# Stick-breaking attention: two key chunks' output products in one run, and transposed weights written over the untransposed ones

## The chip, the cores and the metric

The program runs on one core of one Trainium2 chip. The metric is the device time of one execution, in microseconds (us), given as the median of several runs. The profile shows five engines: PE (TensorE, whose weight loads are listed as PEld), DVE (VectorE), ACT (ScalarE), POOL (GpSimd) and SP (SyncE, which here only issues DMAs). Each engine runs its own list of instructions in the order in which the program was built.

## The reference, cut to what matters

The kernel computes two blocks, one after the other, on 2048 tokens of width 1024. The first block has a gated short convolution and then an attention layer whose weights break a stick; the second block has a pooling mixer and an attention over 256 selected keys per query. The change is in the first block's attention:

```
for blk in range(n_blocks):                       # 128 queries each
    z = einsum(q_blk, k[:kl]) * HEAD_DIM ** -0.5  # 8 heads of 64
    mask = arange(kl)[None, :] < q_pos[:, None]
    log_one_minus = where(mask, log_sigmoid(-z), 0.0)
    rev = cumsum(log_one_minus, axis=3, reverse=True)
    weights = exp(where(mask, z + rev, -inf))
    outs.append(einsum(weights, v[:kl]))
```

So the weight of a key is sigmoid(z) of that key times the product of sigmoid(-z) over all later keys that the query sees. The keys are therefore walked from the last one back to the first.

## The kernel before, in words

The work is written as Python generators, one for each phase: `phase_a` is the convolution, `phase_b` makes keys, values, queries and gates, `phase_c` is the stick-breaking attention, `phase_d` the projection after it, `phase_e` and `phase_e2` the second block's projections, `phase_f` its attention, `phase_g` the output. `merge` interleaves two generators: the one whose share of its own stated total is lowest goes next, so a smaller total makes a generator look further along and be called less often. `ahead` gives all that a generator emits a higher priority. What is written in this way goes through a scheduler, which sets the order on each engine; that order then is fixed. `phase_c(0)` (queries 0 to 1023) is merged with `phase_b(1)`, and `phase_c(1)` (queries 1024 to 2047) with `phase_d(0)`, `phase_e(0)` and `phase_e2`. Most of the work beside phase_c is the helper `lin`, whose matmuls L119, L120 and L121 stream 512 columns each.

In `phase_c`, p is a pair of heads, g a group of 512 queries, i one of its four blocks of 128 queries, and c a chunk of 512 keys, from g down to 0. nb is the number of 128-key pieces of a chunk: 4, or i+1 in the diagonal chunk c == g. For each (p, g, i, c), here called a chunk, and each head a of the pair:

- L533 and L534 (PE) make the scores z in one of two PSUM banks.
- L536 (ACT) writes sigmoid(z) into a buffer `s` of the ring `cs` (4 buffers before). In the diagonal chunk L538 and L541 (DVE) mask and form 1-s; elsewhere L543 (ACT) writes sigmoid(-z) into `e` of the ring `ce`.
- L546 (DVE) runs the product of `e` backwards over the keys, and starts from the last value of the chunk done before. L547 (DVE), and L549 (POOL) for one column, multiply it into `s`: these are the weights.
- L553 (PE) transposes `s` in nb pieces of 128x128 into a PSUM tile `tp`, and L555 (ACT) copies that into a buffer `wt` (ring of 3).

When both heads are copied, L561 (PE) adds the chunk's output products to the bank `o`: 2 nb matmuls, whose outputs lie in partitions 0 to 63 for the first head and 64 to 127 for the second. Each of them loads only 64 columns of stationary data (the values) and stands in the profile as two records, so a chunk of four pieces has 8 matmuls and 16 records. The helper `burst` lets the first of them wait for the last copy and gives them one priority, so that they tend to stand in one run. For each p, the groups g = 0, 1, 2, 3 have 4, 8, 12 and 16 chunks: 48 chunks in `phase_c(0)`, 112 in `phase_c(1)`, 160 in all.

At the end of a group L576 (DVE) multiplies `o` by the gate `sg`, and a DMA stores it to `ogd`. All `crf` names in the profile are buffers of the rings above; `crr` holds queries and keys.

Of the kernel before, what the change touches and what calls it, by code (L numbers as in the profile page):

```python
# [7 lines left out]
F32 = mybir.dt.float32  # L8
# [7 lines left out]
ALU = mybir.AluOpType  # L16
# [39 lines left out]
def merge(*gens):  # L56
    run(merged(*gens))
# [11 lines left out]
class Build:  # L69
# [434 lines left out]
    def phase_c(self, h):  # L504
        nc = self.nc
        if h == 0:
            self.c_rings()
        for p in range(4):
            for g in (2 * h, 2 * h + 1):
                gs = slice((g % 2) * CH, (g % 2 + 1) * CH)  # L510
                sg = self.turn("csg", 1)
                self.dma(sg, self.sg1[p][h][:, gs])
                q = [self.load_dup("cq", 3, self.qst[p][h], a, gs) for a in range(2)]
                kt, vt = {}, {}
                for c in range(g, -1, -1):
                    cs = slice((c % 2) * CH, (c % 2 + 1) * CH)
                    kt[c] = self.load_stack("ck", 4, self.kst[p][c // 2], cs)
                    if c == g or c % 2:
                        n = HT // P if c % 2 else HT // P // 2
                        v = self.turn("cv", 2)  # L520
                        self.dma(v[:, :n], self.vst[p][c // 2][: n * P, :].rearrange("(b p) d -> p b d", p=P))
                    vt[c] = v[:, c % 2 * 4 : c % 2 * 4 + 4]
                o = self.psum("o")
                for i in range(4):
                    qs = slice(i * P, (i + 1) * P)
                    prev = [None, None]
                    for c in range(g, -1, -1):
                        nb = i + 1 if c == g else 4
                        W = nb * P
                        wts = []  # L530
                        for a in range(2):
# [3 lines left out]
                            s = self.turn("cs", 4)  # L535
# [15 lines left out]
                            tp = self.psum("tp")  # L551
                            for j in range(nb):
                                nc.tensor.transpose(tp[:, j * P : (j + 1) * P], s[:, j * P : (j + 1) * P], self.ident)  # L553
                            wt = self.turn("wt", 3)
                            last = nc.scalar.copy(wt[:, :W], tp[:, :W])  # L555
                            wts.append(wt)
                        with self.burst(last) as first:
                            for j in range(nb):
                                for a in range(2):
                                    first(  # L560
                                        nc.tensor.matmul(  # L561
                                            o[a * 64 : (a + 1) * 64, qs],
                                            vt[c][:, j, a * 64 : (a + 1) * 64],
# [916 lines left out]
```

## Time and profile before

| what | value |
|---|---|
| median of 3 runs | 3356.41 us (3351.19 to 3359.43) |
| the profiled execution's own time | 3360.51 us |
| its span, first to last instruction | 3358.8 us |
| PE busy | 3212.6 us, 96% |
| DVE busy | 2249.0 us, 67% |
| ACT busy | 1501.3 us, 45% |
| POOL busy | 470.9 us, 14% |
| mean granted TensorE clock | 0.977 of full |

A busy PE here is a PE with a matmul in flight, and matmuls overlap: one of 512 columns lasts 0.39 us in the records, while the next starts 0.23 us after it. So the distance between starts is what a matmul costs, and the busy share does not show how much of it is useful.

### The profile page before, as it was taken

How to read it: one execution, taken by the hardware profiler on the slowest of the kernel's cores; microseconds unless marked ns; L12 is line 12 of the kernel's file. 1: busy time of each engine (PE TensorE's matmuls, PEld its weight loads, DVE VectorE, ACT ScalarE, POOL GpSimd, SP SyncE). 2: the span in 40 equal slices, each digit the busy share in tenths (PEclk: the TensorE clock that was granted, in tenths of full speed). 3: DMA queues.
4: the chain of work that ended last, by engine and by line, in shares of the span. 5: the costliest groups of instructions: out<-in, count | busy, mean ns of one | idle time of the engine just before them, and what ended most of it. 6: DMA issues, size and time to landing. Idle time of an engine off the chain costs nothing.

```text
span 3358.8 us, 49679 instructions
## 1 busy us (share of the span) xinstructions
PE 3212.6 (96%) x18050; PEld 2546.6 (76%) x18050; DVE 2249.0 (67%) x4516; ACT 1501.3 (45%) x2794; POOL 470.9 (14%) x584
## 2 busy tenths in 40 slices
PE   8999999999999999998899999889999999999997
PEld 7888888788878778776678887667877777666775
DVE  5344534545253878788888788798946878799741
ACT  4111421111232544465555555565365555776571
POOL 0000010000100000033312112331110143103002
PEclk9999999999999999997999999889999999999998
DMA  3111452424454455474456544554553265115115
GB/s 105 48 48 47 138 169 88 132 85 138 129 179 154 143 153 160 127 245 131 117 157 182 171 141 158 168 168 135 172 164 105 84 214 171 47 39 172 46 30 180
DMA packets 371683, 439.77 MB, mean 131 GB/s; under 512 B 25696, under 2 KB 271968, under 8 KB 371424
## 3 DMA queue, kind: packets, MB, share of 16 engines
q1 hardware_dynamic: 371424, 436.44, 42.1%
q8 instruction: 147, 2.41, 0.3%
q14 instruction: 112, 0.92, 0.1%
HBM read 309.46 MB, written 125.30 MB: 129 GB/s over the span
## 4 chain that ended last, share of the span: by engine, by line
PE 78%; DVE 13%; ACT 3%; issue 3%; DMA 2%; POOL 0%; SPq 0%; ACTq 0%; DVEq 0%; POOLq 0%
PE lin L119 11%; PE lin L120 10%; PE lin L121 10%; PE z L119 4%; PE z L120 4%; PE z L121 4%; PE o L561 4%; PE o L1221 3%; PE tp L553 3%; PE tp L1213 3%; PE tp L120 3%; PE tp L119 3%; PE tp L121 3%; DVE crf L546 2%; PE z L533 2%
## 5 line engine op out<-in xcount | busy, mean ns | idle before, releaser
L119 PE MATMUL lin<-act,fixedr 128*128 128x512 f32 x1488 | 597.4, 402 | 15.0 <-DVE x1r L597 7.9
L120 PE MATMUL lin<-act,fixedr 128*128 128x512 f32 x1488 | 595.2, 400 | 9.5 <-DVE act L618 7.2
L121 PE MATMUL lin<-act,fixedr 128*128 128x512 f32 x1488 | 592.2, 398 | 0.0
L104 ACT ACTIVATE fixedr<-fixed 128x512 fp32r<-128x512 f32 x294 | 185.9, 634 | 726.1 <-PE lin L120 263.2
L546 DVE TENSOR_TENSOR_SCAN crf<-crf 128x512 f32<-128x512 f32 (+3 forms) x320 | 354.6, 1116 | 74.0 <-ACT crf L543 71.4
L119 PEld LDWEIGHTS lin<-act,fixedr 128*128 128x128 f32 x1488 | 284.0, 191 | 80.3 <-DVE x1r L597 9.8
L120 PEld LDWEIGHTS lin<-act,fixedr 128*128 128x128 f32 x1488 | 283.8, 191 | 74.3 <-DVE act L618 10.0
L105 DVE TENSOR_TENSOR fixedr<-fixed,fixedr 128x512 fp32r<-128x512 f32 x294 | 203.5, 693 | 197.7 <-ACT fixedr L104 186.2
L121 PEld LDWEIGHTS lin<-act,fixedr 128*128 128x128 f32 x1488 | 283.7, 191 | 61.0 <-issue 0.2
L1162 DVE CUSTOM_DVE_ANT_0 fe<-z,masks 128x512 f32<-128x512 f32 (+3 forms) x320 | 188.3, 605 | 105.0 <-PE tp L1213 53.3
L119 PE MATMUL z<-act,fixedr 128*128 128x512 f32 x584 | 231.7, 397 | 9.3 <-ACT fixedr L104 9.3
L536 ACT ACTIVATE crf<-z 128x512 f32<-128x512 f32 (+3 forms) x320 | 175.3, 549 | 144.6 <-PE tp L553 109.8
L555 ACT COPY crf<-tp 128x512 f32<-128x512 f32 (+3 forms) x320 | 164.9, 532 | 156.0 <-PE tp L553 135.8
L120 PE MATMUL z<-act,fixedr 128*128 128x512 f32 x584 | 231.0, 396 | 0.0
L121 PE MATMUL z<-act,fixedr 128*128 128x512 f32 x584 | 230.9, 396 | 0.0
L549 POOL TENSOR_TENSOR crf<-crf 128x1 f32<-128x1 f32 x192 | 93.2, 487 | 928.8 <-ACT crf L536 732.5
L1176 ACT ACTIVATE fe<-fe,fixed 128x1024 f32<-128x1024 f32 (+7 forms) x192 | 189.7, 992 | 71.6 <-DVE fixed L1173 70.8
L1215 ACT COPY ff<-tp 128x512 f32<-128x512 f32 (+3 forms) x320 | 161.2, 523 | 127.2 <-PE o L1221 65.7
L883 DVE SCALAR_TENSOR_TENSOR sc<-ff,fixed,sc 128x512 f32<-128x512 f32 (+3 forms) x266 | 180.8, 702 | 52.3 <-ACT ff L876 50.5
L547 DVE TENSOR_TENSOR crf<-crf 128x511 f32<-128x511 f32 (+3 forms) x320 | 199.8, 630 | 10.7 <-PE lin L121 0.5
L1213 PE MATMUL tp<-fixed,fe 128*128 128x128 f32 x1088 | 181.8, 282 | 21.0 <-ACT fe L1176 16.4
L876 ACT ACTIVATE ff<-z 128x512 f32<-128x512 f32 (+3 forms) x304 | 158.2, 547 | 92.2 <-PE z L874 73.1
(346 smaller groups left out, 6541.5 us busy)
## 6 DMA issues: line engine op xcount, KB each, us to landing
fixed<-in_w_in_a_dram SPq DMA_DIRECT2D x128, 256.0 KB, 2.7
fixedr<-kept_w_out SPq DMA_DIRECT2D x64, 512.0 KB, 4.8
kept_w_in<-fixedr SPq DMA_DIRECT2D x46, 512.0 KB, 4.1
fixedr<-kept_w_in SPq DMA_DIRECT2D x46, 512.0 KB, 4.0
crr<-kst SPq DMA_DIRECT2D x80, 256.0 KB, 5.4
crr<-qst SPq DMA_DIRECT2D x64, 256.0 KB, 5.4
fixed<-x2d SPq DMA_DIRECT2D x64, 256.0 KB, 3.8
ffr<-q2s SPq DMA_DIRECT2D x128, 128.0 KB, 2.9
```

What stands on the lines that cost most here:

```text
L104: nc.scalar.activation(t[:, 0], raw, AF.Copy)
L105: nc.vector.tensor_tensor(t[:, 1], raw, t[:, 0].bitcast(F32), ALU.subtract)
L119: self.nc.tensor.matmul(ps[:, :n], whi[k], a, start=k == 0, stop=False)
L120: self.nc.tensor.matmul(ps[:, :n], whi[k], b, start=False, stop=False)
L121: self.nc.tensor.matmul(ps[:, :n], wlo[k], a, start=False, stop=k == nk - 1)
L536: nc.scalar.activation(s[:, :W], z[:, :W], AF.Sigmoid)
L546: nc.vector.tensor_tensor_scan(er, er, er, left, ALU.mult, ALU.min)
L547: nc.vector.tensor_tensor(s[:, : W - 1], s[:, : W - 1], e[:, 1:W], ALU.mult)
L883: nc.vector.scalar_tensor_tensor(sc[:, c0 : c0 + m], r[:, :m], w, sc[:, c0 : c0 + m], ALU.mult, ALU.add)
L1162: nc.vector.tensor_tensor_reduce(row[c0 // HT][:, c0 % HT : c0 % HT + m], z[:, :m], mb[:, c0 : c0 + m], 1.0, NEG, ALU.subtract, ALU.max, m ...
L1176: nc.scalar.activation(x, x, AF.Exp, bias=nbs, scale=sc, accum_out=den[:, u, hd : hd + 1])
L1213: nc.tensor.transpose(tp[:, j * P : (j + 1) * P], pe[a][k0 // HT][:, k0 % HT : k0 % HT + P], self.ident)
```

## The change

Each chunk's transposes, copies and output products are moved into a method `c_outputs`, which is called one chunk later, when the next chunk's scores and weights have been emitted (`c_behind` holds what is due). The copy L579 writes the transposed weights back into `s` itself, so the ring `wt` is gone and `cs` has 7 buffers. The output products are collected in `c_due` and issued for two chunks together, when g - c is odd or c is 0. The loads of the gate and of the values of a group are written behind the first chunk of that group. Two totals of the interleaving change: `phase_c(1)` from 260 to 230, and the last part of `phase_f` from 500 to 460.

```
-        f = self.at.tile([P, (4 + 4 + 3) * CH + 2 * HT + CH], F32, name="crf", tag="crf", bufs=1)
+        f = self.at.tile([P, (7 + 4) * CH + 2 * HT + CH], F32, name="crf", tag="crf", bufs=1)
...
-        for name, b, m in (("cs", 4, CH), ("ce", 4, CH), ("wt", 3, CH), ("csg", 1, CH), ("cv", 2, HT)):
+        for name, b, m in (("cs", 7, CH), ("ce", 4, CH), ("csg", 1, CH), ("cv", 2, HT)):
...
+        self.c_behind, self.c_out, self.c_due = None, {}, []
...
-                            s = self.turn("cs", 4)
+                            s = self.turn("cs", 7)
...
-                            tp = self.psum("tp")
-                            for j in range(nb):
-                                nc.tensor.transpose(tp[:, j * P : (j + 1) * P], s[:, j * P : (j + 1) * P], self.ident)
-                            wt = self.turn("wt", 3)
-                            last = nc.scalar.copy(wt[:, :W], tp[:, :W])
-                            wts.append(wt)
-                        with self.burst(last) as first:
-                            for j in range(nb):
-                                for a in range(2):
-                                    first(
...
+                            ws.append(s)
+                        if self.c_behind is not None:
+                            self.c_outputs(*self.c_behind)
+                        if (i, c) == (0, g):
+                            sg = self.turn("csg", 1)
+                            self.dma(sg, self.sg1[p][h][:, gs])
+                            for k in range(g, -1, -1):
+                                if k == g or k % 2:
...
+                        self.c_behind = h, p, g, i, c, ws, vt[c], sg
...
+    def c_outputs(self, h, p, g, i, c, ws, v, sg):
...
+        for s in ws:
+            tp = self.psum("tp")
+            for j in range(nb):
+                nc.tensor.transpose(tp[:, j * P : (j + 1) * P], s[:, j * P : (j + 1) * P], self.ident)
+            last = nc.scalar.copy(s[:, :W], tp[:, :W])
+        self.c_due += [(a, ws[a], j, v, c == g and j == 0, c == 0 and j == nb - 1) for j in range(nb) for a in range(2)]
+        if (g - c) % 2 or c == 0:
+            o = self.c_out[p, g]
+            with self.burst(last) as first:
+                for a, wt, j, v, begins, ends in self.c_due:
+                    first(
+                        nc.tensor.matmul(
...
+            self.c_due = []
+        if (i, c) == (3, 0):
+            nc.vector.tensor_tensor(sg, o, sg, ALU.mult)
+            self.dma(self.ogd[p][h][:, (g % 2) * CH : (g % 2 + 1) * CH], sg)
...
-            merge((self.ahead(self.phase_c(1), 2000), 260), (de, 300))
+            merge((self.ahead(self.phase_c(1), 2000), 230), (de, 300))
...
-            merge((self.ahead(f, 0), 500), (fill, 400))
+            merge((self.ahead(f, 0), 460), (fill, 400))
```

In the changed program's lines, L527 and L528 are the scores (before: L533, L534), L530 and L537 the sigmoids (L536, L543), L540 and L541 the running product and the weights (L546, L547), L578 the transposes (L553), L579 the copy (L555) and L586 the output products (L561).

The first place is on PE in the middle of `phase_c(1)`, where 1920 to 1935 of the L119 matmuls have been issued; `act` and `fixedr` are the operands of `lin`. Before, one chunk's eight output products stand in one run:

```order
L119 MATMUL lin<-act_10634,fixedr 128x512
L120 MATMUL lin<-act_10635,fixedr 128x512
L561 MATMUL o<-crf 64x128 x8
L553 MATMUL tp<-fixed,crf 128x128 x8
L533 MATMUL z<-crr 128x512
L534 MATMUL z<-crr 128x512
```

Now a run there holds those of two chunks:

```order
L119 MATMUL lin<-act_10542,fixedr 128x512
L120 MATMUL lin<-act_10543,fixedr 128x512
L121 MATMUL lin<-act_10542,fixedr 128x512
L578 MATMUL tp<-fixed,crf 128x128 x2
L586 MATMUL o<-crf 64x128 x16
L578 MATMUL tp<-fixed,crf 128x128 x4
L119 MATMUL lin<-act_10544,fixedr 128x512
L120 MATMUL lin<-act_10545,fixedr 128x512
```

The number of output matmuls is the same in all, 1088 in phase_c, and the transposes are too; what moved is how they are strung together. The second place is on ACT at the end of `phase_c(1)`, where the last chunks are done. Before, the copy of a transposed chunk follows each head's pair of sigmoids:

```order
L555 COPY crf<-tp 128x512
L536 ACTIVATE crf<-z 128x512
L543 ACTIVATE crf<-z 128x512
L555 COPY crf<-tp 128x512 x5
L876 ACTIVATE ff<-z 128x384
```

Now several sigmoids stand ahead of several copies:

```order
L530 ACTIVATE crf<-z 128x512 x2
L537 ACTIVATE crf<-z 128x512 x2
L530 ACTIVATE crf<-z 128x512
L579 COPY crf<-tp 128x512
L530 ACTIVATE crf<-z 128x512
L537 ACTIVATE crf<-z 128x512 x2
L579 COPY crf<-tp 128x512 x3
```

A copy is thus queued behind sigmoids of later chunks. The third place is SP's queue of DMA issues in the first half of `phase_c(1)`, where `vst` holds values, `sg` gates and `ogd` the outputs that are stored. Before:

```order
L77 DMA crf<-vst_1_161 128x4x128
L77 DMA fixed<-x2d_140 128x512 x5
L77 DMA crf<-vst_0_160 128x8x128
L77 DMA fixed<-in_w_in_dram 128x4x128
L77 DMA kept_w_in_0_11239<-fixedr 128x1024
L77 DMA ogd_1_175<-crf 128x512
L77 DMA crf<-sg_1_169 128x512
```

Now:

```order
L77 DMA crf<-vst_1_161 128x4x128
L77 DMA fixed<-x2d_140 128x512 x3
L77 DMA fixed<-in_w_in_dram 128x4x128
L77 DMA kept_w_in_0_11111<-fixedr 128x1024
L77 DMA crf<-vst_0_160 128x8x128
L77 DMA ogd_1_175<-crf 128x512
L77 DMA sw<-xe 32x1024 x2
L77 DMA crf<-sg_1_169 128x512
```

Although the loads of values and gates are written later in the code, they stand at nearly the same place of the queue: the second load of values went behind two other DMAs, and the gate behind a pair.

## Rows read from the trace of the kernel before

**Rows 1.** The page, part 1: busy time, share, instructions of two engines.

```profile
PE 3212.6 (96%) x18050; PEld 2546.6 (76%) x18050; DVE 2249.0 (67%) x4516; ACT 1501.3 (45%) x2794; POOL 470.9 (14%) x584
```

**Rows 2.** Busy time in five stretches; columns: length, engines, clock, DMA share, GB/s.

```profile
1089.00:1516.00 427.00, 413.37 (x2524) 326.59 (x2523) 346.12 (x579) 206.97 (x424) 51.21 (x66) 0.99 0.55 165
1516.00:1673.00 157.00, 135.79 (x864) 105.34 (x863) 131.37 (x187) 88.34 (x170) 49.09 (x58) 0.86 0.45 125
1673.00:2045.00 372.00, 369.58 (x2393) 298.00 (x2392) 303.94 (x429) 207.50 (x403) 52.74 (x98) 1.00 0.54 162
2045.00:2156.00 111.00, 97.14 (x620) 74.12 (x619) 82.41 (x112) 59.05 (x112) 26.19 (x49) 0.92 0.42 131
2156.00:3359.00 1203.00, 1124.47 (x6971) 870.34 (x6969) 895.53 (x2534) 685.99 (x1297) 243.33 (x234) 0.97 0.40 127
```

**Rows 3.** The chain that ended last, by line, from 1700 to 2060 us.

```profile
by line: PE lin L121 18.9%; PE lin L119 18.9%; PE lin L120 18.9%; PE o L561 14.5%; PE tp L553 14.1%; PE z L534 6.6%; PE z L533 6.5%; PE lin L671 1.6%; issue 0.0%
```

**Rows 4.** The same from 1440 to 1700 us.

```profile
by line: DVE crf L546 15.2%; issue 11.7%; PE o L561 7.2%; PE tp L553 6.8%; DVE crf L547 5.9%; PE lin L119 5.2%; PE lin L120 5.1%; PE lin L121 5.0%; DMA fixed<-x2d 4.0%; PE z L533 3.5%; PE z L534 3.1%; DVE act L618 2.8%; PE lin L129 2.4%; DV
```

**Rows 5.** Timeline of PE: start, time in flight, instruction; a run of 16 records.

```profile
1720.07 0.39 PE L120 MATMUL lin<-act,fixedr 128*128 128x512 f32 x1
1720.39 1.09 PE L561 MATMUL o<-crf 128*64 128x128 f32 x16
1721.41 1.11 PE L553 MATMUL tp<-fixed,crf 128*128 128x128 f32 x8
1722.27 0.47 PE L533 MATMUL z<-crr 128*128 128x512 f32 x1
1722.59 0.39 PE L534 MATMUL z<-crr 128*128 128x512 f32 x1
```

**Rows 6.** The same view: two transposes between matmuls of 512 columns.

```profile
1704.04 0.39 PE L120 MATMUL lin<-act,fixedr 128*128 128x512 f32 x1
1704.27 0.38 PE L553 MATMUL tp<-fixed,crf 128*128 128x128 f32 x2
1704.40 0.48 PE L121 MATMUL lin<-act,fixedr 128*128 128x512 f32 x1
1704.72 0.39 PE L119 MATMUL lin<-act,fixedr 128*128 128x512 f32 x1
```

**Rows 7.** The same view: a run of 2 records, and one of 12.

```profile
1713.01 0.43 PE L561 MATMUL o<-crf 128*64 128x128 f32 x2
1713.38 0.33 PE L553 MATMUL tp<-fixed,crf 128*128 128x128 f32 x1
...
1741.74 0.88 PE L561 MATMUL o<-crf 128*64 128x128 f32 x12
1742.55 1.10 PE L553 MATMUL tp<-fixed,crf 128*128 128x128 f32 x8
```

**Rows 8.** PE's wait in phase_c, 1673 to 2045 us: total us, times, longest.

```profile
PE tp L553 <- ACT crf L543: 0.8, 1, 0.8
```

**Rows 9.** PE's longest wait of phase_c, 1516 to 1673 us.

```profile
PE tp L553 <- DVE crf L547: 9.7, 7, 4.9
```

**Rows 10.** PE's longest wait of phase_c, 1100 to 2140 us.

```profile
PE tp L553 <- DVE crf L547: 11.1, 9, 4.9
```

**Rows 11.** ACT's wait before a sigmoid, 1100 to 2140 us.

```profile
ACT crf L536 <- PE tp L553: 109.8, 60, 5.9
```

**Rows 12.** Groups by line and shape: count, busy us, mean ns, idle before, releasers.

```profile
L546 DVE TENSOR_TENSOR_SCAN crf<-crf 128x512 f32<-128x512 f32 x224 | 287.8, 1290 | 72.1 <-ACT crf L543 71.4
L547 DVE TENSOR_TENSOR crf<-crf 128x511 f32<-128x511 f32 x224 | 158.6, 712 | 8.7 <-PE lin L121 0.5
L536 ACT ACTIVATE crf<-z 128x512 f32<-128x512 f32 x224 | 137.4, 615 | 68.3 <-PE tp L553 60.2 <-issue 5.0 <-DVE fixed L418 2.5
L543 ACT ACTIVATE crf<-z 128x512 f32<-128x512 f32 x192 | 117.3, 612 | 4.2 <-DVE crf L546 4.2
```

**Rows 13.** DMA issues from 1090 to 2140 us: KB each, median us to landing.

```profile
crf<-sg SPq DMA_DIRECT2D x15, 256.0 KB, 3.0
```

More of the change, by code (lines that the diff above doesn't have):

```diff
@@ L517, in phase_c @@
                     kt[c] = self.load_stack("ck", 4, self.kst[p][c // 2], cs)
[L518 to L523, printed above, removed]
+                self.c_out[p, g] = None
                 for i in range(4):
@@ L529, in phase_c @@
                         W = nb * P
-                        wts = []
+                        ws = []
                         for a in range(2):
@@ L550, in phase_c @@
                             prev[a] = e
-                            tp = self.psum("tp")
-                            for j in range(nb):
-                                nc.tensor.transpose(tp[:, j * P : (j + 1) * P], s[:, j * P : (j + 1) * P], self.ident)
-                            wt = self.turn("wt", 3)
-                            last = nc.scalar.copy(wt[:, :W], tp[:, :W])
-                            wts.append(wt)
-                        with self.burst(last) as first:
-                            for j in range(nb):
-                                for a in range(2):
-                                    first(
-                                        nc.tensor.matmul(
-                                            o[a * 64 : (a + 1) * 64, qs],
-                                            vt[c][:, j, a * 64 : (a + 1) * 64],
-                                            wts[a][:, j * P : (j + 1) * P],
-                                            start=(c == g and j == 0),
-                                            stop=(c == 0 and j == nb - 1),
-                                        )
-                                    )
+                            ws.append(s)
[6 more added lines that the diff above has]
+                                if k == g or k % 2:
+                                    n = HT // P if k % 2 else HT // P // 2
+                                    v = self.turn("cv", 2)
+                                    self.dma(v[:, :n], self.vst[p][k // 2][: n * P, :].rearrange("(b p) d -> p b d", p=P))
+                                vt[k] = v[:, k % 2 * 4 : k % 2 * 4 + 4]
+                        self.c_behind = h, p, g, i, c, ws, vt[c], sg
                         yield 0.65 * nb
@@ L575, in phase_c @@
                         nc.gpsimd.tensor_copy(self.mark, s[:, 0:1])
-                nc.vector.tensor_tensor(sg, o, sg, ALU.mult)
-                self.dma(self.ogd[p][h][:, gs], sg)
+        self.c_outputs(*self.c_behind)
+        self.c_behind = None
+    def c_outputs(self, h, p, g, i, c, ws, v, sg):
+        nc = self.nc
+        nb = i + 1 if c == g else 4
+        W = nb * P
+        if self.c_out[p, g] is None:
+            self.c_out[p, g] = self.psum("o")
+        for s in ws:
[10 more added lines that the diff above has]
+                        nc.tensor.matmul(
+                            o[a * 64 : (a + 1) * 64, i * P : (i + 1) * P],
+                            v[:, j, a * 64 : (a + 1) * 64],
+                            wt[:, j * P : (j + 1) * P],
+                            start=begins,
+                            stop=ends,
+                        )
+                    )
+            self.c_due = []
+        if (i, c) == (3, 0):
+            nc.vector.tensor_tensor(sg, o, sg, ALU.mult)
+            self.dma(self.ogd[p][h][:, (g % 2) * CH : (g % 2 + 1) * CH], sg)
     def phase_d(self, h, pool):
```

2 lines of the change are left out of this document (removed).

## The prediction

> **What bounds the kernel now.** I read the page first: PE is busy 96% of the span, DVE 67% [rows 1]. That share cannot say what a change on PE is worth, so I cut the span at the stretches in which phase_c runs and asked for the busy time in each. In two long ones, 427 us and 372 us, PE is busy 97% and 99% at full clock, while DVE is at 81% and 82%. In two short ones, 157 us and 111 us, PE is busy only 86% and 88%, its clock falls to 0.86 and 0.92 of full, and in the first of them DVE is at 84% [rows 2]. Then the chain that ended last: from 1700 to 2060 us all of it lies on PE, with `lin`, scores, transposes and output products as its links [rows 3]. From 1440 to 1700 us its longest link is the running product on DVE [rows 4]. So time taken off PE in the two long stretches (799 us together) shows in the end; in the short ones it mostly does not, because PE there waits for weights: 9.7 us in seven waits in the first [rows 9], of 11.1 us in all of phase_c [rows 10].
>
> **The price of a run of output products.** Two matmuls of 512 columns start 0.23 us apart, and two transposes put between such matmuls add 1704.72 - 1704.27 - 0.23 = 0.22 us, so 0.11 each, and no more for being set apart [rows 6]. Output products are dearer than their own number. Ahead of a run of 16 records (one full chunk) the L120 takes 0.32 instead of 0.23 us: 0.09 more. The run takes 1.02 us. The eight transposes behind it and the L533 take 1.18 us, where 8 x 0.11 + 0.23 = 1.11 would do: 0.07 more. Together the run costs 1.18 us [rows 5]. A run of 12 records takes 0.81 us, so 4 records are 0.21 and one is 0.0525 us; a run of 2 takes 0.37, far above 2 x 0.0525 [rows 7]. The 16 records are thus worth 0.84 us, and **0.34 us is the price of having a run at all**, paid at its two ends.
>
> **What the change does to the runs.** I count runs in the order of PE's instructions before and now (a run is a stretch of 64-row outputs without anything else in between; phase_f's L1221 and L1204 have the same form). The whole program goes from 421 runs to 350, that is 71 fewer, and L561 alone from 188 to 127. By place, with the edges of [rows 2] (they are the starts of the 1500th, 1850th, 1900th, 2200th and 2250th L119, by which the two orders are laid side by side):
>
> - 1089 to 1516 us: 73 runs, now 53: 20 x 0.34 = 6.8 us
> - 1516 to 1673 us: 27, now 12: 15 x 0.34 = 5.1 us
> - 1673 to 2045 us: 63, now 41: 22 x 0.34 = 7.5 us
> - 2045 to 2156 us: 25, now 21: 4 x 0.34 = 1.4 us
> - later, in phase_f: 233, now 223: 10 x 0.34 = 3.4 us
>
> I take the first and third whole, 14.3 us, because PE is the chain there. Of the other three, 9.9 us, I take half, 4.9 us: PE is the bound in parts of each only, and in the 2156 to 3359 stretch it is busy 93% [rows 2]. That is 19.2 us; bounds for it are 14.3 (nothing counts where PE waits) and 24.1 us (all of it).
>
> **Rule against row.** The row prices a run, not a matmul: 0.37 us for 2 records against 0.81 for 12 [rows 7]. The Trainium skill (TensorEngine Tiling (Array Packing), Instruction Overhead) says that each matmul carries a fixed overhead of about 60 cycles. By that rule alone joining runs is worth nothing, since 1088 products stay 1088 products; by the rows it is worth 24.1 us at most. The trace contradicts the rule as the whole account.
>
> **What else is moved.** Transposes, copies, sigmoids, running products and multiplications keep their number and shapes, so DVE's and ACT's sums stay. The copy now writes `s` instead of `wt`; both are in SBUF, with the same shape: nothing. The loads of gates and values are written later, but SP's order has them one or two DMAs further back at most; a gate lands in 3.0 us [rows 13] and is needed only at its group's end, and PE shows no wait for values. If that cover went, 16 gate loads of 3.0 us would be 48 us; I see no place for it and take 0. The totals 230 and 460 hardly move the work: the first and last L533 have nearly the same position among PE's instructions in both orders. I take 0, between a gain and a loss of some 5 us, about what one of phase_c's longest waits costs (4.9 us, [rows 9]).
>
> **The wait that the change adds.** A buffer of `cs` was free again when its transposes were done. Now it is free when the run of its pair is done, up to a chunk later, with 7 buffers instead of 4. The sigmoid that wants the buffer waits on ACT, and behind it stand copies of older chunks, for which the joined run waits. ACT already spends 109.8 us in 60 such waits, 1.8 us each [rows 11], yet PE waits for a sigmoid once, 0.8 us, in the third stretch [rows 8], so the long stretches have slack. In the short ones there is little. From sigmoid to weights is 0.615 + 0.612 + 1.290 + 0.712 = 3.23 us [rows 12], which bounds the price of one missed pair from above; from below it is nothing, and less than nothing if the delay by a chunk removes the 11.1 us of waits. I take two more waits of the average size 9.7 / 7 = 1.4 us [rows 9], 3 us.
>
> **Sum.** 19.2 - 3 = 16.2 us. The profiled execution took 3360.5 us, so 3344.3 us on its scale; it was 4.1 us above the median of the runs, so I forecast the median: 3356.4 - 16.2 = **3340 us**.
>
> **Rivals.**
>
> 1. *Chains give back what the runs save.* In the two short stretches 19 runs go away by joining. Each joined run is 16 records longer for whoever waits behind it, 0.84 us [rows 5, 7]; 19 x 0.84 = 16 us back against 14.3 + 4.9 us saved: 3353 us, within 3346 to 3359. For: DVE leads the chain there [rows 4]. Against: a weight that waits for DVE does not care how long PE's run is.
> 2. *The ring stops ACT: slower.* The Trainium skill (TensorE: Matmul & The Clock Gate, Architectural detail) says that ACT's queue is strictly first in, first out; the rows agree only in that nothing passes a waiting L536. Where a sigmoid waits for a joined run, the copies behind it are late, and then that run's successors. At 3.23 us a pair [rows 12], six pairs eat the 19.2 us, and nine make the kernel slower by 10 us. There are 64 pairs; twelve missed ones would cost 39 us: 3376 us. For: the sigmoids' waits are there already [rows 11]. Against: three more buffers, and almost no such wait reaches PE in the long stretches [rows 8].
> 3. *All of it counts, and the waits go too.* 24.1 + 11.1 = 35 us: 3321 us. For: transposes come a chunk later, so weights are ready. Against: the scheduler puts the scores later as well, and DVE stays as loaded.
> 4. *The price is by matmul (the page's rule), so the joining does nothing*: 3356 us. Against: [rows 5, 7].
>
> **Chances.** The forecast has 0.54, with a range of its own of 3330 to 3346 us; rival 1 has 0.20, rival 2 0.09, rival 3 0.13, rival 4 0.04. The measurement of this kernel can tell about 0.3% from no change, 10 us: below 3346.3 is faster, above 3366.5 slower. The forecast and rival 3 make faster, 0.67; rivals 1 and 4 make no change, 0.24; rival 2 makes slower, 0.09. For a range that leaves out 2 in 10 I go from rival 3's 3321 to the upper edge of rival 1: 3320 to 3359 us.
>
> **What would show it.** Right: the changed profile has runs of 28 to 32 records of L586 that take 0.18 + 32 x 0.0525 = 1.9 us, and about 60 fewer runs; PE's time in the two long stretches falls by 6 to 8 us each; DVE's and ACT's busy sums stay within a few us; the short stretches keep their length to about 5 us. Wrong price: a run of 32 records takes as long as two of 16, 2.04 us and its ends as much as before. Rival 2: waits of L530 for L586 on ACT, and waits of PE's L586 for L579 or of L578 for DVE above 25 us in sum. The forecast fails if the clock falls for longer in the short stretches than now, or if a new place appears where PE waits for phase_c after 2156 us, since phase_d(1) and phase_f begin only when its last group is stored.

## The result and the profile after

The changed kernel took 3337.47 us (median, 3335.70 to 3343.63 in 7 runs); the kernel before, run beside it, 3359.43 us (3351.19 to 3367.78 in 7 runs). The ratio is 0.9945, with a 95% interval of 0.993 to 0.996: 13 to 23 us less, where the forecast was 16.2 us less (3340 us, range 3320 to 3359). The profiled spans differ by 3358.8 - 3339.4 = 19.4 us.

The page of the changed kernel, part 1, which answers to [rows 1]:

```profile
span 3339.4 us, 49666 instructions
PE 3186.8 (95%) x18050; PEld 2541.3 (76%) x18050; DVE 2225.3 (67%) x4516; ACT 1509.4 (45%) x2796; POOL 491.6 (15%) x584
```

Split the span into PE's busy time and its idle time. Busy fell from 3212.6 to 3186.8, by 25.8 us, with the same 18050 instructions. Idle is span minus busy: it rose from 146.2 to 152.6, by 6.4 us. Busy time also depends on the clock, whose mean was 0.980 of full in this execution and 0.977 in the one before. Busy time times clock, busy time at full clock from here on, went from 3138.7 to 3123.1 us. So 15.6 of the 25.8 us are cheaper work, some 10 us are the higher clock, and 6.4 us were lost again in waits. This split carries the rest of the study.

Busy time by stretch in the changed kernel, cut at the same L119 marks as [rows 2]; columns: stretch, its length, PE, PEld, DVE, ACT, POOL, clock, DMA share, GB/s:

```profile
1090.00:1514.00 424.00, 411.44 (x2571) 331.45 (x2570) 339.25 (x587) 214.88 (x432) 62.81 (x67) 0.99 0.56 166
1514.00:1650.00 136.00, 114.47 (x796) 90.49 (x795) 124.36 (x175) 84.31 (x159) 52.39 (x56) 0.95 0.48 139
1650.00:2017.00 367.00, 362.25 (x2352) 297.27 (x2351) 289.92 (x414) 202.69 (x393) 60.62 (x95) 0.99 0.53 162
2017.00:2137.00 120.00, 104.57 (x675) 78.61 (x674) 91.68 (x128) 65.53 (x124) 25.38 (x53) 0.93 0.43 132
2137.00:3340.00 1203.00, 1121.81 (x6974) 871.24 (x6972) 890.49 (x2535) 688.34 (x1301) 242.10 (x234) 0.97 0.40 127
```

Against [rows 2] PE's busy time falls by 1.9 us in the first stretch, 21.3 in the second, 7.3 in the third and 2.7 in the last, and rises by 7.4 in the fourth. Work moved between the stretches: the first and the fourth now hold more of PE's records (2571 instead of 2524, and 675 instead of 620), the second and the third fewer (796 instead of 864, and 2352 instead of 2393).

PE's timeline in the changed kernel, around a run of two joined chunks (start, time in flight, instruction, xcount):

```profile
1716.73 0.40 PE L119 MATMUL lin<-act,fixedr 128*128 128x512 f32 x1
1717.06 1.97 PE L586 MATMUL o<-crf 128*64 128x128 f32 x32
1718.95 0.99 PE L578 MATMUL tp<-fixed,crf 128*128 128x128 f32 x7
1719.70 0.47 PE L120 MATMUL lin<-act,fixedr 128*128 128x512 f32 x1
1720.02 0.39 PE L121 MATMUL lin<-act,fixedr 128*128 128x512 f32 x1
```

The 32 records take 1718.95 - 1717.06 = 1.89 us. Ahead of them the L119 takes 0.33 instead of 0.23, and behind them seven transposes and an L120 take 1.07 where 7 x 0.11 + 0.23 = 1.00 would do. Together 1.89 + 0.10 + 0.07 = 2.06 us, against 2 x 1.18 = 2.36 for two runs of 16 [rows 5]: 0.30 us saved at this place.

PE's waits of phase_c in the changed kernel from 1090 to 2137 us (total us, times, longest), which answer to [rows 10]:

```profile
PE tp L578 <- DVE crf L541: 17.0, 17, 3.3
PE z L527 <- ACT crf L537: 4.5, 6, 2.5
PE tp L578 <- ACT crf L579: 4.3, 6, 1.5
PE o L586 <- ACT crf L579: 3.3, 6, 0.9
```

The wait of transposes for weights is longer in sum than before (17.0 against 11.1 us), in more and shorter pieces: the longest is 3.3 us where it was 4.9.

ACT's waits there (1100 to 2137 us), which answer to [rows 11]:

```profile
ACT crf L530 <- PE o L586: 75.9, 67, 6.5
ACT crf L530 <- PE z L528: 45.4, 42, 3.8
```

The sigmoids no longer wait for transposes but for the joined runs, as rival 2 said. PE's waits for an ACT result in the fence of PE's waits are 12.1 us together. Before, from 1090 to 2155 us, they were 6.2 us:

```profile
PE tp L553 <- ACT crf L543: 2.0, 2, 1.2
PE z L533 <- ACT crf L543: 1.9, 2, 1.4
PE o L561 <- ACT crf L555: 1.4, 3, 0.5
PE z L533 <- ACT crf L536: 0.9, 1, 0.9
```

### The profile page after: what moved, and what is told of

Its sections match the earlier page's. It is cut to its first block, busy times and chain, and to the rows that moved or that the text cites. A ratio compares the mean times of both kernels' runs of the same rounds, so it can differ in the third digit from the quotient of the medians.

```text
span 3339.4 us, 49666 instructions
## 1 busy us (share of the span) xinstructions
PE 3186.8 (95%) x18050; PEld 2541.3 (76%) x18050; DVE 2225.3 (67%) x4516; ACT 1509.4 (45%) x2796; POOL 491.6 (15%) x584
## 5 line engine op out<-in xcount | busy, mean ns | idle before, releaser
L120 PE MATMUL lin<-act,fixedr 128*128 128x512 f32 x1488 | 595.4, 400 | 14.2 <-DVE act L638 11.0
L119 PE MATMUL lin<-act,fixedr 128*128 128x512 f32 x1488 | 594.4, 401 | 11.3 <-ACT act L81 3.9
L540 DVE TENSOR_TENSOR_SCAN crf<-crf 128x512 f32<-128x512 f32 (+3 forms) x320 | 348.6, 1105 | 47.7 <-ACT crf L537 45.9
L120 PEld LDWEIGHTS lin<-act,fixedr 128*128 128x128 f32 x1488 | 281.3, 189 | 78.4 <-DVE act L638 15.8
L119 PEld LDWEIGHTS lin<-act,fixedr 128*128 128x128 f32 x1488 | 281.9, 189 | 73.2 <-DVE x1r L617 5.6
L543 POOL TENSOR_TENSOR crf<-crf 128x1 f32<-128x1 f32 x192 | 111.8, 587 | 878.6 <-ACT crf L530 500.4
L119 PE MATMUL z<-act,fixedr 128*128 128x512 f32 x584 | 231.9, 398 | 9.3 <-ACT fixedr L104 9.3
L120 PE MATMUL z<-act,fixedr 128*128 128x512 f32 x584 | 231.3, 397 | 0.0
L530 ACT ACTIVATE crf<-z 128x512 f32<-128x512 f32 (+3 forms) x320 | 167.7, 541 | 122.9 <-PE o L586 75.9
L579 ACT COPY crf<-tp 128x512 f32<-128x512 f32 (+3 forms) x320 | 163.2, 534 | 125.9 <-PE tp L578 111.7
L896 ACT ACTIVATE ff<-z 128x512 f32<-128x512 f32 (+3 forms) x304 | 156.9, 545 | 100.8 <-PE z L894 79.6
L541 DVE TENSOR_TENSOR crf<-crf 128x511 f32<-128x511 f32 (+3 forms) x320 | 198.4, 632 | 4.8
L578 PE MATMUL tp<-fixed,crf 128*128 128x128 f32 x1088 | 178.1, 283 | 22.1 <-DVE crf L541 17.0
```

The costliest lines, as they stand in the source:

```text
L119: self.nc.tensor.matmul(ps[:, :n], whi[k], a, start=k == 0, stop=False)
L120: self.nc.tensor.matmul(ps[:, :n], whi[k], b, start=False, stop=False)
L530: nc.scalar.activation(s[:, :W], z[:, :W], AF.Sigmoid)
L540: nc.vector.tensor_tensor_scan(er, er, er, left, ALU.mult, ALU.min)
L541: nc.vector.tensor_tensor(s[:, : W - 1], s[:, : W - 1], e[:, 1:W], ALU.mult)
```

## The experiments

All kernels were run in 5 rounds beside the kernel before. The table has the runs of 64-row outputs counted in the order of PE's instructions, the medians and ratios, and from the profiled execution of each the page's PE busy time, the mean granted clock and PE's idle time (span minus busy). The clock is given to 0.001, which is 3 us of busy time, so differences of 3 us in the column "busy at full clock" are not read. Each ratio is to the kernel before as it ran beside that kernel, whose median went from 3357.07 to 3359.43 us between these comparisons; medians of different rows can differ by that much on their own.

| kernel | runs | median us | ratio, 95% | busy | clock | busy at full clock | idle |
|---|---|---|---|---|---|---|---|
| before | 421 | 3359.43 | 1 | 3212.6 | 0.977 | 3138.7 | 146.2 |
| the change | 350 | 3337.47 | 0.9945 (0.993 to 0.996) | 3186.8 | 0.980 | 3123.1 | 152.6 |
| e1 one-chunk runs | 418 | 3352.62 | 0.999 (0.9976 to 1.0003) | 3205.6 | 0.979 | 3138.3 | 147.9 |
| e12 one-chunk runs, 234 | 413 | 3357.21 | 0.9997 (0.9986 to 1.0007) | 3199.5 | 0.982 | 3141.9 | 152.9 |
| e2 pairs at once | 342 | 3367.52 | 1.0036 (1.0023 to 1.0049) | 3190.7 | 0.977 | 3117.3 | 176.1 |
| e7 pairs at once, 215 | 328 | 3353.57 | 0.998 (0.9965 to 0.9995) | 3191.4 | 0.975 | 3111.6 | 166.8 |
| e3 in place alone | 435 | 3361.87 | 1.0014 (1.0004 to 1.0023) | 3212.1 | 0.979 | 3144.6 | 151.2 |
| e4 old total of phase_f | 353 | 3340.47 | 0.9957 (0.9944 to 0.997) | 3192.8 | 0.977 | 3119.4 | 154.6 |
| e11 totals 286, 480 | 371 | 3353.45 | 0.9992 (0.9982 to 1.0001) | 3192.2 | 0.980 | 3128.4 | 158.7 |
| e6 three chunks | 334 | 3340.74 | 0.9938 (0.9918 to 0.9958) | 3178.6 | 0.981 | 3118.2 | 157.8 |
| e5 all chunks in phase_f | 326 | 3374.19 | 1.0041 (1.0028 to 1.0053) | 3194.4 | 0.976 | 3117.7 | 178.7 |
| e10 pairs in phase_f | 348 | 3343.05 | 0.996 (0.9946 to 0.9974) | 3184.9 | 0.981 | 3124.4 | 152.3 |
| e9 two chunks late | 359 | 3316.63 | 0.9873 (0.9857 to 0.989) | 3177.3 | 0.984 | 3126.5 | 138.0 |

How far one execution differs from another can be read from four kernels. The change, e4, e5 and e10 have the same 6390 PE records in the same order from the 1500th to the 2250th L119 (they differ in phase_f alone). In their four profiled executions this stretch took 1047.5, 1052.6, 1052.9 and 1047.6 us, and PE's idle time in it was 54.3, 54.5, 53.5 and 58.0 us. So idle times that differ by less than 5 us are not told apart below.

A straight line through the thirteen pairs of runs and busy time at full clock (least squares) rises by 0.27 us per run, with a standard error of 0.02 and a correlation of 0.97. The number of runs alone, against the spans, has a correlation of 0.16: what the runs save on PE's busy time is often lost in its idle time.

Most totals differ between these kernels so that each kernel's buffers fit in SBUF. The change with 260 and 500, and the kernel before with 230 and 460, were not run.

**e1, the pairs taken out.** The delay, the copy in place and the ring of 7 stay.

```
-        if (g - c) % 2 or c == 0:
+        if True:
...
-            merge((self.ahead(self.phase_c(1), 2000), 230), (de, 300))
+            merge((self.ahead(self.phase_c(1), 2000), 256), (de, 300))
...
-            merge((self.ahead(f, 0), 460), (fill, 400))
+            merge((self.ahead(f, 0), 440), (fill, 400))
```

> The change without its pairing: outputs a chunk later, copies in place, ring of 7, but every chunk has its own run (418 runs of 64-row outputs in the whole order, 421 before, 350 in the change; interleaving totals 256 and 440, so that the program fits on the chip's memory). Theory A, each run has a price of 0.34 us: 3 fewer runs, 1 us, so the time of the kernel before, ratio 0.998 to 1.002. Theory B, most of the gain came from the delay by a chunk, which shortened PE's waits for weights in the stretch after 1516 us and kept the clock up there (its length fell from 157 to 137 us in the change): some 14 of the 19 us stay, ratio about 0.996.

Measured 0.999: the gain is gone with the pairs. Its idle time is like the kernel before's; its busy time at full clock is 15.2 us above the change's.

**e12, the same with totals nearly the change's own** (234 and 460), because e11, further down, showed that the totals are not neutral.

```
-        if (g - c) % 2 or c == 0:
+        if True:
...
-            merge((self.ahead(self.phase_c(1), 2000), 230), (de, 300))
+            merge((self.ahead(self.phase_c(1), 2000), 234), (de, 300))
```

> The change without its pairs, now with totals 234 and 460, nearly its own 230 and 460 (the first experiment had 256 and 440): each chunk's products stand in a run of their own, with the delay, the ring of 7 and the copy in place. 413 runs, 63 more than the change. If the pairs are what pays, the runs put back 63 x 0.34 = 21 us at most, 10 to 16 us of it on the path, nearly all between 1090 and 2160 us: 3347 to 3354 us, 0.996 to 0.999. If the total of 230 gave the gain and the pairs nothing, it stands as the change: 3335 to 3342 us, 0.994 to 0.995.

0.9997, a little above the range for the pairs and far from the one for the totals. Idle time equals the change's (152.9 and 152.6); the difference is busy time, 18.8 us at full clock for 63 runs, 0.30 each. The pairs are what pays.

**e2, pairs without the delay.** Each chunk's transposes stand behind its own weights.

```
-                        if self.c_behind is not None:
-                            self.c_outputs(*self.c_behind)
...
-                        self.c_behind = h, p, g, i, c, ws, vt[c], sg
+                        self.c_outputs(h, p, g, i, c, ws, vt[c], sg)
...
-            merge((self.ahead(self.phase_c(1), 2000), 230), (de, 300))
+            merge((self.ahead(self.phase_c(1), 2000), 260), (de, 300))
...
-            merge((self.ahead(f, 0), 460), (fill, 400))
+            merge((self.ahead(f, 0), 500), (fill, 400))
```

> Pairing and the copy in place without the delay: a chunk's transposes and copies follow its weights at once, and the products of two chunks are joined; both totals are those of before (260 and 500). 342 runs, 79 fewer than before. Theory A: 79 x 0.34 = 27 us, of which about 0.8 count: 21 us, ratio about 0.994. Theory B: without the delay the stretch after 1516 us stays at about 157 us; what is left is 5 to 8 us, ratio about 0.998.

Both theories missed: the kernel is slower than before, with 79 fewer runs. PE's longest wait of phase_c in e2, 1090 to 2155 us:

```profile
PE tp L574 <- DVE crf L541: 29.4, 24, 5.8
```

L574 are its transposes. They wait 29.4 us for weights, against 11.1 before [rows 10] and 17.0 with the delay. That is 12.4 of the 23.5 us of idle time that e2 has more than the change; what the rest waits for was not worked out.

**e7, the same with totals 215 and 460**, which leaves fewer runs still.

```
-                        if self.c_behind is not None:
-                            self.c_outputs(*self.c_behind)
...
-                        self.c_behind = h, p, g, i, c, ws, vt[c], sg
+                        self.c_outputs(h, p, g, i, c, ws, vt[c], sg)
...
-            merge((self.ahead(self.phase_c(1), 2000), 230), (de, 300))
+            merge((self.ahead(self.phase_c(1), 2000), 215), (de, 300))
```

> Pairs and the copy in place, but each chunk's transposes and products stand at once behind its weights, as in the second experiment, with totals 215 and 460: 328 runs, 22 fewer than the change. If the number of runs set the time, it would be 7 us below the change, a ratio of 0.9925. If the delay of a chunk is what lets the pairs pay (theory A), the transposes wait for the last of the vector engine's work on their weights for 25 us or more, about twice as many waits as with the change, and the time is that of the kernel before or above it: 1.000 to 1.004.

It landed between the two: 0.998, with the lowest busy time at full clock of the thirteen (3111.6 us), and 166.8 us idle. PE's two longest waits in e7, 1090 to 2150 us:

```profile
PE tp L574 <- DVE crf L541: 18.6, 21, 3.0
PE tp L574 <- ACT crf L575: 7.7, 9, 3.2
```

The first is smaller than the 25 us expected; the second, for the copy L575 of the tile before, is not among the waits before, and the change has 4.3 us of it. So without the delay the pairs bring 14 to 24 us more idle time than the change has, in either kernel.

**e3, neither pairs nor delay**, only the copy in place and the ring of 7.

```
-                        self.c_behind = h, p, g, i, c, ws, vt[c], sg
+                        self.c_outputs(h, p, g, i, c, ws, vt[c], sg)
...
-        if (g - c) % 2 or c == 0:
+        if True:
...
-            merge((self.ahead(self.phase_c(1), 2000), 230), (de, 300))
+            merge((self.ahead(self.phase_c(1), 2000), 205), (de, 300))
```

> Neither pairing nor delay: only the copy in place with a ring of 7 (total of phase_c(1) 205 so that it fits). 435 runs, 14 more than before. Theory A: 14 x 0.34 x 0.8 = 4 us slower, ratio about 1.001. Theory B: no delay, no gain, 1.000. A third theory, that the larger ring (7 instead of 4) is what helps, gives some of the 19 us here: 0.996 or less.

1.0014, as theory A said of its 14 runs more: the buffers by themselves give nothing.

**e4, phase_f's total back at 500.**

```
-            merge((self.ahead(f, 0), 460), (fill, 400))
+            merge((self.ahead(f, 0), 500), (fill, 400))
```

> The change with phase_f's total set back from 460 to 500; 353 runs against the change's 350. Theories A and B: the same time as the change, ratio 0.994 to 0.996. If the total of 460 were part of the gain, the ratio would be above 0.997.

0.9957, the change's 0.9945 within the intervals: this total is not the gain.

**e5, the same idea in phase_f**, whose outputs are late already: all chunks of a head pair in one run, and the weights `fe` written over in place.

```
-                wt = self.turn("fwt", 3)
-                last = nc.scalar.copy(wt[:, : nb * P], tp[:, : nb * P])
+                wt = pe[a][c * CH // HT][:, c * CH % HT : c * CH % HT + nb * P]
+                last = nc.scalar.copy(wt, tp[:, : nb * P])
...
-            with self.burst(last) as first:
+            due += [(c, j, a, wts[a]) for j in range(nb) for a in range(2)]
+            if c == nch - 1:
+                with self.burst(last) as first:
```

> The change, and in phase_f too: the products of all chunks of a query block and head pair stand in one run, and its transposed weights overwrite the untransposed ones. 326 runs of 64-row outputs where the change has 350. Theory A (a run costs 0.34 us wherever TensorE is the chain, and phase_f's outputs are already taken one head pair late, so no wait for weights is added): 24 x 0.34 = 8 us at most, 4 to 8 us off the change, a ratio to the kernel before of 0.992 to 0.9935. Theory B (a longer run waits for the copy of its last chunk, and that wait gives the saving back, as in the kernel without the delay): no faster than the change, 0.9945 to 0.997.

Slower by 37 us than the change by the medians (32 us by the ratios), more than theory B allowed. Of 33.7 us between the spans, 26.1 are idle time; PE's busy time is 7.6 longer at the lower clock, though at full clock it is 5.4 shorter. Much of the idle time comes late. PE's longest waits in e5 from 3095 to 3375 us, where little work is left but phase_f's own:

```profile
PE o L1243 <- ACT fe L1236: 14.8, 9, 2.9
PE lin L119 <- DMA fixedr<-kept_w_out: 9.1, 4, 6.5
PE tp L1234 <- ACT fe L1236: 7.0, 5, 4.1
```

The first and third are joined runs and transposes that wait for the copy L1236. In the changed kernel such waits there are 1.3 and 1.2 us.

**e10, only two chunks a run in phase_f**, in place too: as e5, with the condition `if c % 2 or c == nch - 1`.

```
+            if c % 2 or c == nch - 1:
+                with self.burst(last) as first:
```

> The change, and in phase_f runs of two chunks (in place of all chunks of a head pair, as in the fifth experiment), with its weights overwritten in place. 348 runs, 2 fewer than the change. If the fifth experiment lost its time because a longer run waits for more copies of the scalar engine while little else is left for TensorE after 3100 us, two chunks wait for one more copy in place of up to three: a third to a half of its loss of 37 us, 3350 to 3360 us, 0.998 to 1.001. If the copy in place is what it lost by, at any length: as the fifth, 3370 to 3376 us. If neither (the number of runs alone): as the change, 0.9945.

0.996, as the change; the waits of e5 are down to 2.0 us:

```profile
PE lin L119 <- DMA fixedr<-kept_w_out: 10.5, 3, 7.3
PE o L1243 <- ACT fe L1236: 1.8, 4, 0.8
...
PE tp L1234 <- ACT fe L1236: 0.2, 1, 0.2
```

So neither the copy in place nor a run of two is what e5 lost by. What is left is the length of its runs, and with it the wait for the last copy.

**e6, up to three chunks a run in phase_c**, ring of 9, totals 206 and 480.

```
-                            s = self.turn("cs", 7)
+                            s = self.turn("cs", 9)
...
-        if (g - c) % 2 or c == 0:
+        if g - c == 2 or c == 0:
```

> The change with runs of up to three chunks in place of two, a ring of 9, totals 206 and 480. 334 runs where the change has 350. Theory A (price of a run times their number, the delay of a chunk kept): 16 x 0.34 = 5 us off the change, 0.993. Theory B (a run's length also costs: more products stand back to back, and the scores that the sigmoids wait for stand behind them): as the change or up to 5 us above it, 0.9945 to 0.996.

0.9938, with an interval that reaches into both theories. Its busy time at full clock is 4.9 us lower and its idle time 5.2 us higher than the change's, both near what one execution can differ by.

**e8 and e9, outputs two chunks late.** In e8 the values and the gate of a group were loaded one chunk too early, over those that a late chunk still needed; this changes the computation, and the program then also took its path of exact selection (4947.86 us). Nothing is read from its time.

> The change with outputs two chunks late in place of one, a ring of 9, totals 284 and 480: 366 runs, 16 more than the change. If the delay pays because the transposes no longer wait for the weights, a second chunk takes most of the waits that are left (about 17 us of transposes behind L541 in the changed kernel) and puts 16 x 0.34 = 5 us of runs in: 3325 to 3335 us by that theory, 0.990 to 0.993. If one chunk is all the slack that counts, the runs alone decide: 3340 to 3345 us, 0.995 to 0.997.

In e9 the loads come a chunk later (ring of 9, totals 290 and 480):

```
-                        if self.c_behind is not None:
-                            self.c_outputs(*self.c_behind)
-                        if (i, c) == (0, g):
+                        if len(self.c_behind) == 2:
+                            self.c_outputs(*self.c_behind.pop(0))
+                        late += 1
+                        if late == 2:
...
-                        self.c_behind = h, p, g, i, c, ws, vt[c], sg
+                        self.c_behind.append((h, p, g, i, c, ws, vt, sg))
```

> The change with outputs two chunks late, a ring of 9, totals 290 and 480; v and the gate are loaded one chunk later, once the last late chunk of the group before has used them. 359 runs, 9 more than the change. If the delay pays because the transposes no longer wait for the weights, the second chunk takes most of the 17 us of transposes behind L541 that the changed kernel still has between 1090 and 2137 us, and the runs put 9 x 0.34 = 3 us in: 3325 to 3332 us, 0.990 to 0.992. If one chunk is all the slack that counts, the runs decide: 3340 to 3343 us, 0.995 to 0.996.

3316.63 us, 0.9873: below both ranges, and 21 us below the change by the medians, the fastest kernel of the study. Its PE waits of phase_c from 1090 to 2142 us:

```profile
PE z L527 <- ACT crf L537: 7.0, 6, 4.4
PE tp L579 <- DVE crf L541: 7.0, 9, 1.8
```

The transposes wait 7.0 us for weights (17.0 in the change), never longer than 1.8 us. Over the whole span idle time is 138.0 us, 14.6 less than the change's, and the clock is 0.984, against 0.980. Its busy time at full clock is 3.4 us above the change's, so what e9 gains is idle time and clock. More runs than the change (359 to 350), and still faster. The second chunk of delay came with a ring of 9 and later loads; these were not run apart.

**e11, the control for e9's totals**: the change with 286 and 480.

```
-            merge((self.ahead(self.phase_c(1), 2000), 230), (de, 300))
+            merge((self.ahead(self.phase_c(1), 2000), 286), (de, 300))
...
-            merge((self.ahead(f, 0), 460), (fill, 400))
+            merge((self.ahead(f, 0), 480), (fill, 400))
```

> The change with totals 286 and 480 and nothing else: outputs one chunk late, ring of 7. It is the control of the kernel with outputs two chunks late, whose totals are 290 and 480. 371 runs, 21 more than the change. If the second chunk of delay gave that kernel its 21 us, this one stands at the change or up to 7 us above it by its runs: 3337 to 3345 us, 0.9945 to 0.997. If the totals gave them, it stands with that kernel: 3314 to 3325 us, 0.987 to 0.990.

0.9992, above both ranges. So the totals did not give e9 its time; they cost. At the 2250th L119 the kernel is level with the change (2137.77 and 2137.49 us); the loss comes later, 11.1 us more from there to the last PE instruction (1200.4 against 1189.3). PE's longest waits in e11 from 2229 to 2407 us, the stretch in which it falls, and then the change's in the same place, 2227 to 2390 us:

```profile
PE lin L724 <- DVE ff L1251: 7.7, 1, 7.7
PE tp L1233 <- ACT fe L1196: 5.2, 2, 4.4
```

```profile
PE lin L120 <- DVE act L638: 4.9, 3, 3.2
PE lin L119 <- ACT act L637: 2.8, 1, 2.8
```

One wait for the gate multiply of phase_f and two for its weights, 12.9 us, where the change waits 7.7 us for others. The stretch is 178 us long in e11 and 163 in the change. Which of the two totals costs was not run apart; phase_f's at 500 does not (e4).

## Why the forecast came out

**The sum was right, and its parts less so.** Forecast -16.2 us as +3 - 19.2; in the profiled executions PE's idle time rose by 6.4 and its busy time fell by 25.8. Of the 25.8 us 15.6 are work, which I had at 19.2, and some 10 are the clock, for which the sum had no term. Over all executions on record the mean clock is 0.980 with the change and 0.978 to 0.979 in the kernel before, beside whichever kernel it ran, so a part of this gain is in the median too. That work smaller and waits larger than forecast left a total so near to it is luck: the clock made up for both.

**The price of a run**, 0.34 us from [rows 5, 7], is confirmed in size: 0.30 at the place shown above, and 0.27 by the line through all kernels, each of which removes or adds other runs. 71 runs at 0.27 are 19 us at full clock. That the price is by run and not by matmul is shown by e1 and e12, where all products stay and the time goes back. Rival 4 falls. The Trainium skill (TensorEngine Tiling (Array Packing), Instruction Overhead) gives each matmul an overhead of about 60 cycles; by that alone the change would have stood at 1.000 as e1 and e12 do, and its 0.9945 does not agree. That it is 0.27 and not 0.34 on average was not followed up.

**Which runs count** was mis-sized. I counted the short stretches and phase_f by half, since PE waits there for others. The fitted 19 us is what the whole count gives at the fitted price; the forecast's 19.2 us is a price a fifth too high times a count a fifth too low, and that these cancel is luck too. The step's fault was to treat PE's waiting as cover. PE's idle time in the two short stretches is 21.2 and 13.9 us before [rows 2] and 21.5 and 15.4 us in the changed kernel, so cheaper work shortened these stretches as well.

**Where it came** was wrong. I expected 6 to 8 us less PE time in each of the two long stretches; it was 1.9 and 7.3, with 47 records more in the first and 41 fewer in the third, so neither number is the price of its runs alone. And I expected the short ones to keep their length to 5 us; the second stretch went from 156.9 to 136.5 us. Busy time times clock tells what that was: 135.79 x 0.86 = 116.8 us before [rows 2] and 114.47 x 0.95 = 108.7 us now. So 8 of the 21.3 us of busy time are work, of which the forecast's 15 runs at 0.34 us are 5 and the rest is work that moved to other stretches; 13 us are the clock. The fourth stretch became 9.5 us longer, since work moved into it. Three rows of busy time by window, first of the kernel before, then of the changed one, then of e4 (columns as above, the granted clock is the third number from the end):

```profile
1533.00:1557.00 24.00, 20.36 (x97) 17.76 (x97) 17.17 (x23) 7.41 (x15) 8.63 (x8) 0.51 0.23 77
```

```profile
1521.00:1527.00 6.00, 3.71 (x15) 3.00 (x16) 6.00 (x9) 3.41 (x6) 2.55 (x5) 0.74 0.10 40
1527.00:1600.00 73.00, 59.99 (x434) 46.03 (x434) 70.95 (x103) 46.35 (x88) 22.27 (x20) 0.97 0.55 159
```

```profile
1521.00:1545.00 24.00, 21.50 (x108) 19.08 (x110) 17.98 (x24) 9.90 (x18) 11.71 (x8) 0.51 0.28 99
```

Before, PE waited 4.87 us for L547 up to 1536.64 us, and from about 1533 us its clock stood at half, 1.2 of 2.4 GHz, for 24 us. In the changed kernel it stood at half there for some 3 us. But e4, which has nearly the same waits at this place (1.5 and 1.7 us; the change 2.0 and 1.7), stood at half for 24 us in its profiled execution. The same order ran in e5 and e10 too. The whole second stretch in e4, e5 and e10:

```profile
1513.00:1655.00 142.00, 123.50 (x797) 100.07 (x796) 124.52 (x174) 84.46 (x159) 50.51 (x57) 0.87 0.47 134
```

```profile
1513.00:1655.00 142.00, 123.23 (x796) 98.04 (x795) 124.48 (x174) 84.22 (x159) 53.90 (x57) 0.88 0.48 134
```

```profile
1512.00:1647.00 135.00, 113.78 (x798) 89.62 (x797) 124.91 (x175) 84.43 (x159) 55.80 (x57) 0.96 0.49 141
```

Two of the four executions of this order took 142 us here and two 135 to 137, so some 6 of the 20 us are an accident of one execution. How often each length occurs in the executions that were not profiled is not known; e4's profiled execution took 3349.12 us, 8.7 us more than its median.

Where the wait of 4.87 us came from shows in the timeline of the kernel before, 1528 to 1545 us (start, time, instruction, and in brackets the idle time before it):

```profile
1530.34 5.60 POOL L307 TENSOR_TENSOR acc<-acc,sq 128x1024 f32<-128x1024 f32 x2
1530.90 2.85 DVE L105 TENSOR_TENSOR fixedr<-fixed,fixedr 128x512 fp32r<-128x512 f32 x1
...
1533.67 2.82 DVE L547 TENSOR_TENSOR crf<-crf 128x511 f32<-128x511 f32 x1
...
1536.64 1.09 PE L553 MATMUL tp<-fixed,crf 128*128 128x128 f32 x4 [4.87 <-DVE crf L547]
```

DVE did not pause here; two of its multiplications took 2.85 and 2.82 us while POOL added two tiles of 128x1024 (L307). Of the 224 multiplications L547 of this shape, 221 take at most 0.78 us, with a median of 0.69. The three that take 2.6 to 2.8 us all start while an L307 runs on POOL. In the changed kernel four of them take 2.6 to 2.7 us, all inside an L307, and the waits of 2.0 and 1.0 us at 1521.50 and 1530.85 us are right behind two of these.

**The added wait** I had at 3 us, and idle time rose by 6.4; since one execution can differ by some 5 us from another, the two agree no better than that. Its place was mostly wrong. I had it in the ring of `cs`, through sigmoids that wait for joined runs. These waits are there (75.9 us on ACT), and few of them reach PE through the weights: of PE's 17 waits for weights, followed back through the trace, three (0.9, 1.7 and 0.5 us, all after 2090 us) lead to a sigmoid that had waited for L586; the others lead to DVE, which ran without a pause, or to another wait. PE's waits for weights rose by 5.9 us in all, and those for ACT's results by as much, 6.2 to 12.1. Rival 1, the chains give back, names what happened here in small; in e2 it went on to eat the gain whole.

**The delay by a chunk** I had only as a cost, with a remark that it might remove the 11.1 us of waits. This is the step in which the reasoning failed, though the number survived. Idle time with neither pairs nor delay is 151.2 us (e3); with the delay alone 147.9 and 152.9 (e1, e12); with pairs alone 176.1 and 166.8 (e2, e7); with both 152.6, 154.6 and 158.7 (the change, e4, e11); with pairs and two chunks of delay 138.0 (e9). Pairs without delay save PE's time and lose it in waits; the delay takes the waits back. Rival 3's second half, that waits go too, came true only in e9, with the second chunk.

**The totals** I set at nothing, between a gain and a loss of 5 us. For phase_f's 500 this holds (e4). For 286 and 480, which are not the change's own, it does not: 11 us by the place shown under e11, 16 us by the medians, and thus as much as the change itself. That the gain comes with the joining is shown at totals of 230 and 234 (the change and e12). Whether the change would still gain with the old 260 stays open.

**The sums of the other engines** were to stay within a few us. ACT's rose by 8.1, DVE's fell by 23.7 and POOL's rose by 20.7, with the same number of instructions on DVE and POOL and two more on ACT; the mean DVE instruction became 1% shorter. I did not look for the cause.

## What to carry to other kernels

Split the span into the leading engine's busy and idle time, in the kernel before and in every variant: a change that makes that engine's work cheaper shows in the first wherever it stands, and what the new order costs shows in the second. Multiply the busy time by the granted clock before you compare it, since a clock that is 0.003 higher looks like 10 us of cheaper work here.

Joining runs of column-tiled products (64 of 128 output rows each) is worth some 0.3 us a run here, but only if what feeds the longer run is made earlier: shift the consumer by a step, and measure a second step too, since the second step, with its larger ring and later loads, was worth as much (21 us) as the joining (15 to 20 us). Do not join long runs where little other work is left to fill the wait for the last piece, as at this kernel's end (e5 against e10).

## What the hardware showed unasked

- The granted clock after nearly the same waits (1.5 to 2.0 us, then 1.7 us) in the same PE order was half for 24 us in two executions (e4, e5), and for some 3 and 7 us in two others (the change, e10). One profile does not tell what such a place costs; here it was up to 7 us.
- A DVE multiplication of 128x511 that takes 0.69 us in the median took 2.6 to 2.8 us in nearly every case in which it started during POOL's addition of 128x1024: 3 of 4 in the kernel before, 4 of 4 in the changed one.
- A kernel with 79 fewer runs (e2) and one with 95 fewer (e5) were slower than the kernel before by 0.36% and 0.41%, with PE busy some 20 us less in each.
- The same instructions took other times in another order: the POOL's one-column multiply of phase_c 487 ns on average before and 587 ns after.
